# Read-back sums behind the next eviction, fetched operands behind the weights: an order for ScalarE and VectorE in a hybrid encoder layer

## The chip, the cores and the metric

The kernel runs on one core of a Trainium2 chip. The metric is the time of one execution in microseconds (us), the median of three runs. One further execution was taken by the profiler, and all rows below come from it. PE is TensorE (PEld its weight load), DVE is VectorE, ACT is ScalarE, POOL is GpSimd, SP is SyncE, which here only issues transfers.

## The reference

One layer of a streaming encoder, on 512 prompt tokens and 8 × 16 sample tokens, in float32. The lines that matter, `fox_attend` and `s5_mixer` being the attention and the state-space group:

```python
a = rms_norm(x, g_mix)
proj = a @ w_in                      # 2048 -> q, k, v, forget logits, u
...
attn = fox_attend(q, k_all, v_all, c_all[:, past:], c_all, pos_q, pos_k)
ssm, s_re_new, s_im_new = s5_mixer(u, s_re, s_im, ...)
merged = concatenate([rms_norm(attn, g_attn_out), rms_norm(ssm, g_ssm_out)], -1)
h = x + merged @ w_out               # 2048 x 2048
f = rms_norm(h, g_ffn)
h = h + (silu(f @ w_gate) * (f @ w_up)) @ w_down      # 2048 -> 5632 -> 2048
gate = sigmoid(rms_norm(h, g_ple) @ w_ple_gate)       # 2048 x 2048
h = h + gate * (p_i @ w_ple_proj)
```

Keys, values, log forget values and final states are returned too. The change touches only what comes after `merged`.

## The kernel before, in words

All 640 tokens stand on the free axis and features on the partitions. Each float32 operand is rounded to the matmul's format and its remainder is rounded as well (high and low half), and each product is three matmuls: high by high, high by low, low by high (L1243 to L1245). The part after attention and state space consists of products of the four large weight matrices with the activations: o0 to o7 (w_out), g0, u0, g1, u1, ... to u21 (w_gate, w_up), d0 to d25 (w_down, its sum over 5632 cut into pieces), p0 to p7 (w_ple_gate). Every one makes 256 output features and is computed by a seven-product scheme for 2 × 2 blocks in place of eight block products. Its sum runs over units of 512 input features; a unit is 42 matmuls of 128 × 128 weights on 320 tokens. Products o, g, u and p have four units, a d product two, three or four.

Per unit, the ring `Ring` loads 512 KB of weights on SP's queue into a staging tile `wst` (two of them), forms the four block sums `ws` on DVE (L109 to L112), rounds both to the high half `wh` on ACT (L86) and takes the low half `wl` on DVE (L87). `wh` and `wl` have two buffers, so a unit's rounding waits for the last matmul of the unit two before. `next` rounds a unit and the one after it, and `ahead`, at a product's end, the first two of the following product.

A product ends with its eviction from seven of eight PSUM banks (`strassen`): two copies on ACT (`q`, `r12`), six adds on DVE, one on POOL. In the o stage and in the last d products (`last` cells, d18 to d25) `add_h` then adds the result to the residual `o_yT` (a store that accumulates) and reads the sum back as `h`, both on POOL's queue. `done_o` or `done_h`, called one product later, scales `h` by the gain into `c` or `hc` (ACT, L1316), forms three sums of block rows in four adds (DVE, L118 to L121), stores `c` to memory (`fc_dr`, `hc_dr`, on SP's queue) and adds the squares of `h` to the norm's sums (L1291 to L1296). Later `fetch` loads such operands (`kf`, `kt`, `kh`) on POOL's queue, and `cut_next`, called after a unit, rounds one or two of them into high and low half (`cut`: ACT L1085, DVE L1086). The last o product and the last d product do their own: x7 or h5 is read on SP's queue, added on DVE, and scaled straight into the operand; `h5` and `x7` take over a buffer of the pool `R` (two buffers for the results `r`, the sums `h` and these).

On each engine the instructions run in the order that a scheduler fixes when the kernel is built. It works on a timeline that it estimates itself and takes whatever is ready by it, so code that is written later can stand earlier on an engine. `tc.issue_after(ins)`, as a context, keeps an instruction issued within it behind `ins`, on the engine of `ins`; it adds no semaphore. Before the change, none of the functions below uses it.

Of the kernel before, what the change touches and what calls it, by code (L numbers as in the profile page):

```python
# [13 lines left out]
AF = mybir.ActivationFunctionType  # L14
OP = mybir.AluOpType
# [150 lines left out]
def hybrid_step(ctx: ExitStack, tc: tile.TileContext, io):  # L166
    nc = tc.nc
# [23 lines left out]
    ring = Ring(nc, stp, units)  # L191
# [616 lines left out]
    def big(name):  # L808
        return pb_.tile([P, 2, 512], F32, tag="g", name=name, bufs=2)
# [228 lines left out]
    def hrow(j):  # L1038

        return rows(io["o_yT"], j) if j < 7 else rows(h7_dr, 0)  # L1040

    def xrow(j):
        return io["xT"][2 * j : 2 * j + 2]

    for h in range(H):
        if h:
            nc.gpsimd.dma_start(io["o_yT"][2 * (h - 1) * P : 2 * h * P, :].rearrange("(a p) n -> a p n", p=P), xrow(h - 1))
        for which in range(2):
            if h:
                ps = big(f"qk{h}{which}")  # L1050
# [63 lines left out]
    for n in range(8):  # L1114
        ps = big(f"glu{n}")
# [22 lines left out]
    for n in range(KT):  # L1138
# [4 lines left out]
        else:  # L1143
            ps = (two if n % 4 == 1 else big)(f"pj{n}")
# [33 lines left out]
    def pair(name):  # L1178
        return fo.tile([P, 2, NTOK], F32, tag="R", name=name, bufs=2)
# [29 lines left out]
        cut(k, slice(4, 7), x[:, 4:])  # L1209
        return k  # L1210

    uncut, tick = {}, [0]

    def wait_cut(k, x):

# [3 lines left out]
    def fetch(name, slot, dram, i, eng=nc.gpsimd):  # L1219
        k = kp_tile("k" + name, slot)  # L1220
        x = k[:, 1].bitcast(F32)
        eng.dma_start(x, dram[i])
        return wait_cut(k, x)

    def cut_next(n=1, age=2):

        for key in list(uncut)[:n]:
            if tick[0] - uncut[key][0] >= age:
                uncut.pop(key)[1]()

    def products(name, kps, after=None, order=None):

        ps = {i: bank(f"{name}_{i}")[:, :NH2] for i in PRODUCTS}
        n = len(kps) // 2

        def product(i, u, cut):
            a, b = PRODUCTS[i]
            wh, wl = cut
            for c in range(2):
                w = slice(c * P, (c + 1) * P)  # L1240
                k = kps[2 * u + c]
                f, l = u == 0 and c == 0, u == n - 1 and c == 1
                nc.tensor.matmul(ps[i], wh[:, a, w], k[:, 0, b], start=f, stop=False)  # L1243
                nc.tensor.matmul(ps[i], wh[:, a, w], k[:, 1, b], start=False, stop=False)  # L1244
                nc.tensor.matmul(ps[i], wl[:, a, w], k[:, 0, b], start=False, stop=l)  # L1245

        for u in range(n if order is None else n - 2):
            cut = ring.next()
            for k in kps[2 * u : 2 * u + 2]:
                if id(k) in uncut:  # L1250
                    uncut.pop(id(k))[1]()
            for i in PRODUCTS:
                product(i, u, cut)
            tick[0] += 1
            if after is not None:
                after(u)
        if order is not None:
            cuts = [ring.next() for _ in range(2)]
            for i in order:
                for u in range(2):  # L1260
                    product(i, n - 2 + u, cuts[u])
        ring.ahead()
        return ps

    def blocks(r):
        return (r[:, a, b * NH2 : (b + 1) * NH2] for a in range(2) for b in (1, 0))

    def strassen(name, kps, after=None, into=None):
        ps = products(name, kps, after)
        r = pair("r" + name) if into is None else into  # L1270
        r11, r12, r21, r22 = blocks(r)
        q = fo.tile([P, NH2], F32, tag="q", name="q" + name, bufs=1)
        tt = nc.vector.tensor_tensor
        nc.scalar.activation(q, ps[1], AF.Copy)
        tt(r11, q, ps[2], op=OP.add)
        nc.scalar.activation(r12, ps[3], AF.Copy)
        tt(q, q, ps[6], op=OP.add)
        tt(r22, q, ps[7], op=OP.add)
        tt(r12, r12, ps[5], op=OP.add)
        tt(r21, r22, ps[4], op=OP.subtract)  # L1280
        tt(r22, r22, ps[5], op=OP.add)
        nc.gpsimd.tensor_tensor(r12, r12, q, op=OP.add)
        return r

# [5 lines left out]
    def squares(s, x, first):  # L1290
        nc.scalar.activation(x, x, AF.Square)  # L1291
        if first:
            nc.vector.tensor_tensor(s, x[:, 0], x[:, 1], op=OP.add)
        else:
            nc.vector.tensor_tensor(s, s, x[:, 0], op=OP.add)
            nc.vector.tensor_tensor(s, s, x[:, 1], op=OP.add)  # L1296

    def add_h(r, j):

        nc.gpsimd.dma_start(hrow(j), r, accum_op=OP.add)  # L1300
        x = pair(f"h{j}")
        nc.gpsimd.dma_start(x, hrow(j))
        return x
# [7 lines left out]
    ssqh, ssqp = ssqa, ssqs  # L1311
# [6 lines left out]
    fk, due, f6 = [], [], []  # L1318

    def done_o(x, j):  # L1320
        c = seven(f"c{j}")
        scaled(c, x, gffn, j)
        if j < 6:
            keep(nc.vector, c, fc_dr, j)
        else:
            winograd_rows(nc.vector, c[:, :4], c[:, 4:])
            f6.append(c)
        squares(ssqh, x, j == 0)

    for j in range(8):  # L1330
        def after(u, j=j):
            if j == 7:
                if u == 2:
                    due.pop()()
                    due.append(pair("x7"))
                    nc.sync.dma_start(due[0], xrow(7).rearrange("a p n -> p a n"))
                for i in (2 * u, 2 * u + 1):
                    if i < 6:
                        fk.append(fetch(f"f{i}", i, fc_dr, i))
                cut_next(2 if u == 2 else 1, 1)  # L1340

        r = strassen(f"o{j}", mk, after)
        if j < 7 and due:
            due.pop()()
        if j < 7:
            x = add_h(r, j)
            due.append(lambda x=x, j=j: done_o(x, j))
    fk.append(whole(kp_tile("kf6", 6), f6[0]))
    x = due.pop()
# [6 lines left out]

    def after_g0(u, x=x):
        if u == 1:
            squares(ssqh, x, False)
        cut_next(1, 0)  # L1360

    tk, slots = {}, (0, 1, 2, 3, 4, 5, 6, 7)
# [1 line left out]
    def next_t():  # L1364

        u = len(tk) // 2
        if u < FT // 4:
            for i in (2 * u, 2 * u + 1):
                tk[i] = fetch(f"t{i}", slots[i % 8], tc_dr, i)
# [28 lines left out]
    due, h4 = [], []  # L1398

    def done_h(x, j):  # L1400
        c = seven(f"hc{j}")
        scaled(c, x, gple, j)
        if j in (6, 7, 4):
            winograd_rows(nc.vector, c[:, :4], c[:, 4:])
            if j == 4:
                h4.append(c)
            else:
                hk[j] = wait_cut(kp_tile(f"kh{j}", hslot[j]), c)
        else:
            keep(nc.vector, c, hc_dr, j)  # L1410
        squares(ssqp, x, j == 0)

    def next_h(j):
        hk[j] = fetch(f"h{j}", hslot[j], hc_dr, j)

    for n, (j, us, last) in enumerate(cells):
        end = n == len(cells) - 1

        def after(i, us=us, n=n, end=end):
            if end and i == 2:  # L1420
                due.pop()()
            uses[us[i]] -= 1
            if not uses[us[i]] and us[-1] < FT // 4 - 1:
                next_t()
            if n == 0 and not i:
                next_t()
            if end:
                if i == 2:
                    due.append(pair("h5"))
                    nc.sync.dma_start(due[0], hrow(5))  # L1430
                for k in ((0, 1), (2, 3), ())[i]:
                    next_h(k)
            cut_next(1, 1 if n < 2 else 2)

        r = strassen(f"d{n}", [tk[i] for u in us for i in (2 * u, 2 * u + 1)], after)
        if not last:
            nc.gpsimd.dma_start(hrow(j), r, accum_op=OP.add)
        elif not end:
            if due:
                due.pop()()  # L1440
            x = add_h(r, j)
            due.append(lambda x=x, j=j: done_h(x, j))
    hk[4] = whole(kp_tile("kh4", hslot[4]), h4[0])
    x = due.pop()
# [7 lines left out]

    def after_p0(u, x=x):
        if u == 1:
            squares(ssqp, x, False)
        cut_next(1, 0)

    for j in range(7):
# [5 lines left out]
        x = pair(f"pj{j}")  # L1464
# [5 lines left out]
    x = pair("pj7")  # L1470
# [3 lines left out]
    ps = products("p7", hk, order=(1, 2, 6, 5, 3, 7, 4))  # L1474
    z = pair("rp7")
    r11, r12, r21, r22 = blocks(z)
    q = fo.tile([P, NH2], F32, tag="q", name="qp7", bufs=1)
    tt = nc.vector.tensor_tensor
# [141 lines left out]
```

## Time and profile before

| what | value |
|---|---|
| median of 3 runs | 3013.43 us (3011.45 to 3016.4) |
| profiled execution | 3010.09 us, span 3008.0 us, mean granted clock 0.968 |
| TensorE busy | 2857.0 us, 95% of the span |
| VectorE busy | 2198.5 us, 73% |
| ScalarE busy | 1240.8 us, 41% |
| GpSimd busy | 391.3 us, 13% |
| SP's queue (q1) | 326.34 MB in 102880 packets |
| GpSimd's queue (q0) | 109.70 MB in 28240 packets |

The span is the time from the first to the last instruction. The granted clock is TensorE's, 1.00 being the upper of its two levels (2.4 GHz). In the lists of waits and in the timelines, idle time of an engine is put down to what ended it. An engine that waits costs time only where TensorE waits for it in turn.

### The profile page before, as it was taken

The page shows a single profiled execution, that of the slowest core. Times are in us where ns is not written, and L with a number is a line of the kernel's source. Part 1 is how long each engine was busy: PE and PEld are TensorE (multiplying, and loading weights), DVE is VectorE, ACT ScalarE, POOL GpSimd, SP SyncE. Part 2 cuts the span into 40 slices and gives each one's busy share as a digit, 9 for nine tenths or more (in the row PEclk, how much of TensorE's full clock was granted, in tenths as well). Part 3 has the DMA queues.
Part 4 walks back from the last instruction along what each step waited for, and adds up shares of the span by engine and source line. Part 5 has one row for each costly group of instructions (what it writes and reads, how often), then busy time and mean ns, then how long its engine had stood idle before and what let it go on. Part 6 is the DMA issues. An engine that isn't in the chain of part 4 may idle for free. (4 is left out here: it accounts for less than half of the span.)

```text
span 3008.0 us, 47275 instructions
## 1 busy us (share of the span) xinstructions
PE 2857.0 (95%) x19051; PEld 2740.2 (91%) x19051; DVE 2198.5 (73%) x3603; ACT 1240.8 (41%) x1624; POOL 391.3 (13%) x470
## 2 busy tenths in 40 slices
PE   7999999999889889999999999999999999988898
PEld 5889998887889879999999999999999999887798
DVE  7747344445777688888888888888977777767887
ACT  4333355456643453333333333333533334343433
POOL 2213300001001111110111101010111101111000
PEclk9899999999999989999999999999999999999899
DMA  6566634546545623233333233333555455546344
GB/s 226 150 182 192 217 132 163 188 156 238 199 117 165 225 94 115 100 122 100 115 100 121 94 122 103 112 114 108 206 130 169 140 146 159 157 132 194 128 137 125
DMA packets 132635, 443.26 MB, mean 147 GB/s; under 512 B 14000, under 2 KB 34576, under 8 KB 120016
## 3 DMA queue, kind: packets, MB, share of 16 engines
q1 hardware_dynamic: 102880, 326.34, 32.5%
q0 software_dynamic: 28240, 109.70, 13.1%
q10 hardware_dynamic: 1296, 4.20, 0.3%
q8 instruction: 149, 2.44, 0.3%
q14 instruction: 70, 0.57, 0.1%
HBM read 339.96 MB, written 102.16 MB: 147 GB/s over the span
## 5 line engine op out<-in xcount | busy, mean ns | idle before, releaser
L86 ACT ACTIVATE wh<-wst 128x768 fp32r<-128x768 f32 x328 | 276.5, 843 | 615.0 <-issue 284.7
L86 ACT ACTIVATE wh<-ws 128x1024 fp32r<-128x1024 f32 x328 | 345.0, 1052 | 403.6 <-DVE ws L112 403.6
L87 DVE TENSOR_TENSOR wl<-ws,wh 128x1024 fp32r<-128x1024 f32 x328 | 407.5, 1242 | 128.3 <-ACT wh L86 127.6
L87 DVE TENSOR_TENSOR wl<-wst,wh 128x768 fp32r<-128x768 f32 x328 | 329.8, 1005 | 159.7 <-ACT wh L86 159.3
L1243 PE MATMUL d<-kt,wh 128*128 128x320 f32 x1232 | 389.4, 319 | 29.7 <-ACT wh L86 20.4
L1243 PE MATMUL g<-kf,wh 128*128 128x320 f32 x1232 | 382.9, 312 | 16.1 <-ACT wh L86 7.8
L1244 PE MATMUL d<-kt,wh 128*128 128x320 f32 x1232 | 386.2, 317 | 0.0
L1244 PE MATMUL g<-kf,wh 128*128 128x320 f32 x1232 | 381.8, 311 | 0.0
L1243 PE MATMUL u<-kf,wh 128*128 128x320 f32 x1232 | 379.8, 309 | 1.0 <-ACT wh L86 1.0
L1244 PE MATMUL u<-kf,wh 128*128 128x320 f32 x1232 | 379.5, 309 | 0.0
L1245 PE MATMUL g<-kf,wl 128*128 128x320 f32 x1232 | 370.4, 311 | 2.5 <-DVE wl L87 2.5
L1245 PE MATMUL u<-kf,wl 128*128 128x320 f32 x1232 | 368.7, 309 | 0.2 <-DVE wl L87 0.2
L1245 PE MATMUL d<-kt,wl 128*128 128x320 f32 x1232 | 351.4, 317 | 10.8 <-DVE wl L87 10.6
L1243 PEld LDWEIGHTS d<-kt,wh 128*128 128x128 f32 x1232 | 239.6, 195 | 36.8 <-ACT wh L86 25.2
L1243 PEld LDWEIGHTS g<-kf,wh 128*128 128x128 f32 x1232 | 233.3, 189 | 18.5 <-ACT wh L86 9.3
L1245 PEld LDWEIGHTS d<-kt,wl 128*128 128x128 f32 x1232 | 228.0, 193 | 15.6 <-DVE wl L87 15.4
L1244 PEld LDWEIGHTS d<-kt,wh 128*128 128x128 f32 x1232 | 239.8, 195 | 0.0
L1244 PEld LDWEIGHTS g<-kf,wh 128*128 128x128 f32 x1232 | 233.4, 189 | 0.0
L1245 PEld LDWEIGHTS g<-kf,wl 128*128 128x128 f32 x1232 | 229.7, 189 | 3.7 <-DVE wl L87 3.2
L1243 PEld LDWEIGHTS u<-kf,wh 128*128 128x128 f32 x1232 | 231.2, 188 | 2.0 <-ACT wh L86 2.0
L1244 PEld LDWEIGHTS u<-kf,wh 128*128 128x128 f32 x1232 | 231.3, 188 | 0.0
L1245 PEld LDWEIGHTS u<-kf,wl 128*128 128x128 f32 x1232 | 228.1, 188 | 0.6 <-DVE wl L87 0.4
(503 smaller groups left out, 5924.4 us busy)
## 6 DMA issues: line engine op xcount, KB each, us to landing
wst<-in_w_gate SPq DMA_DIRECT2D x88, 512.0 KB
wst<-in_w_up SPq DMA_DIRECT2D x88, 512.0 KB
wst<-in_w_down SPq DMA_DIRECT2D x88, 512.0 KB
tc_dr<-t SPq DMA_DIRECT2D x22, 1120.0 KB
kt<-tc_dr POOLq DMA_DIRECT2D x22, 1120.0 KB, 8.5
wst<-in_w_qk SPq DMA_DIRECT2D x32, 512.0 KB
kc<-in_cache_k SPq DMA_DIRECT2D x16, 1024.0 KB
vc<-in_cache_v SPq DMA_DIRECT2D x16, 1024.0 KB
```

The lines of the kernel that those rows point to most:

```text
L86: a = nc.scalar.activation(wh[:, part], x, AF.Copy)
L87: b = nc.vector.tensor_tensor(wl[:, part], x, wh[:, part].bitcast(F32), op=OP.subtract)
L1243: nc.tensor.matmul(ps[i], wh[:, a, w], k[:, 0, b], start=f, stop=False)
L1244: nc.tensor.matmul(ps[i], wh[:, a, w], k[:, 1, b], start=False, stop=False)
L1245: nc.tensor.matmul(ps[i], wl[:, a, w], k[:, 0, b], start=False, stop=l)
```

## The change

`strassen` now keeps two instructions of its eviction, the second copy on ACT and the last add on DVE. A new helper `behind` runs a function with all that it issues on ACT and DVE kept behind two given instructions. It is used in four places: `done_o` and `done_h` of the previous product run behind the eviction of the product just ended; `cut_next` cuts behind the ring's latest rounding (`ring.done`: ACT's last `wh`, DVE's last `wl`); the same for the last `done_o` and `done_h` in o7 and d25; and for the last squares in g0 and p0.

```diff
@@ -1209,7 +1209,12 @@
         cut(k, slice(4, 7), x[:, 4:])
         return k
 
-    uncut, tick = {}, [0]
+    uncut, tick, evicted = {}, [0], []
+
+    def behind(ins, f):
+
+        with tc.issue_after(ins[0]), tc.issue_after(ins[1]):
+            f()
 
     def wait_cut(k, x):
 
@@ -1226,7 +1231,7 @@
 
         for key in list(uncut)[:n]:
             if tick[0] - uncut[key][0] >= age:
-                uncut.pop(key)[1]()
+                behind(ring.done, uncut.pop(key)[1])
 
     def products(name, kps, after=None, order=None):
 
@@ -1273,12 +1278,13 @@
         tt = nc.vector.tensor_tensor
         nc.scalar.activation(q, ps[1], AF.Copy)
         tt(r11, q, ps[2], op=OP.add)
-        nc.scalar.activation(r12, ps[3], AF.Copy)
+        a = nc.scalar.activation(r12, ps[3], AF.Copy)
         tt(q, q, ps[6], op=OP.add)
         tt(r22, q, ps[7], op=OP.add)
         tt(r12, r12, ps[5], op=OP.add)
         tt(r21, r22, ps[4], op=OP.subtract)
-        tt(r22, r22, ps[5], op=OP.add)
+        b = tt(r22, r22, ps[5], op=OP.add)
+        evicted[:] = a.ins, b.ins
         nc.gpsimd.tensor_tensor(r12, r12, q, op=OP.add)
         return r
 
@@ -1331,7 +1337,7 @@
         def after(u, j=j):
             if j == 7:
                 if u == 2:
-                    due.pop()()
+                    behind(ring.done, due.pop())
                     due.append(pair("x7"))
                     nc.sync.dma_start(due[0], xrow(7).rearrange("a p n -> p a n"))
                 for i in (2 * u, 2 * u + 1):
@@ -1341,7 +1347,7 @@
 
         r = strassen(f"o{j}", mk, after)
         if j < 7 and due:
-            due.pop()()
+            behind(evicted, due.pop())
         if j < 7:
             x = add_h(r, j)
             due.append(lambda x=x, j=j: done_o(x, j))
@@ -1356,7 +1362,7 @@
 
     def after_g0(u, x=x):
         if u == 1:
-            squares(ssqh, x, False)
+            behind(ring.done, lambda: squares(ssqh, x, False))
         cut_next(1, 0)
 
     tk, slots = {}, (0, 1, 2, 3, 4, 5, 6, 7)
@@ -1418,7 +1424,7 @@
 
         def after(i, us=us, n=n, end=end):
             if end and i == 2:
-                due.pop()()
+                behind(ring.done, due.pop())
             uses[us[i]] -= 1
             if not uses[us[i]] and us[-1] < FT // 4 - 1:
                 next_t()
@@ -1437,7 +1443,7 @@
             nc.gpsimd.dma_start(hrow(j), r, accum_op=OP.add)
         elif not end:
             if due:
-                due.pop()()
+                behind(evicted, due.pop())
             x = add_h(r, j)
             due.append(lambda x=x, j=j: done_h(x, j))
     hk[4] = whole(kp_tile("kh4", hslot[4]), h4[0])
@@ -1452,7 +1458,7 @@
 
     def after_p0(u, x=x):
         if u == 1:
-            squares(ssqp, x, False)
+            behind(ring.done, lambda: squares(ssqp, x, False))
         cut_next(1, 0)
 
     for j in range(7):
```

Lines after L1211 move on by five or six. Three places show what becomes of the order. In these rows the number in a name is the unit (wh, ws, wst), the product (qo3, rd7: the eviction's copies) or the operand (c2, h2, kt8).

On ACT, around the eviction of o3 (units 96 to 99; 100 and 101 are the first of o4), before:

```order
L86 ACTIVATE wh98_8568<-ws98_8570 128x1024
L1316 ACTIVATE c2_8757<-h2_8517,c_g_ffn_133 128x640 x2
L86 ACTIVATE wh99_8623<-wst99_8492 128x768
L1291 ACTIVATE h2_8517<-h2_8517 128x1280
L86 ACTIVATE wh99_8623<-ws99_8625 128x1024
L86 ACTIVATE wh100_8678<-wst100_8579 128x768
L1274 ACTIVATE qo3_8747<-o3_1_8519 128x320
L1276 ACTIVATE ro3_8746<-o3_3_8521 128x320
L86 ACTIVATE wh100_8678<-ws100_8680 128x1024
L86 ACTIVATE wh101_8733<-wst101_8634 128x768
```

and after:

```order
L86 ACTIVATE wh99_8623<-wst99_8492 128x768
L86 ACTIVATE wh99_8623<-ws99_8625 128x1024
L86 ACTIVATE wh100_8678<-wst100_8579 128x768
L86 ACTIVATE wh100_8678<-ws100_8680 128x1024
L1279 ACTIVATE qo3_8747<-o3_1_8519 128x320
L1281 ACTIVATE ro3_8746<-o3_3_8521 128x320
L1322 ACTIVATE c2_8757<-h2_8517,c_g_ffn_133 128x640 x2
L1297 ACTIVATE h2_8517<-h2_8517 128x1280
L86 ACTIVATE wh101_8733<-wst101_8634 128x768
L86 ACTIVATE wh101_8733<-ws101_8735 128x1024
```

c2 and the square of h2 stood around wh99 of o3 and now stand behind o3's two copies and in front of wh101.

On ACT, around the eviction of d7 (units 316 to 319 belong to d8, whose third and fourth unit take kt8 to kt11), before:

```order
L1085 ACTIVATE kt8_21902<-kt8_21902 128x1280
L1085 ACTIVATE kt8_21902<-kt8_21902 128x960
L86 ACTIVATE wh316_21965<-wst316_21839 128x768
L86 ACTIVATE wh316_21965<-ws316_21967 128x1024
L1085 ACTIVATE kt9_21904<-kt9_21904 128x1280
L1085 ACTIVATE kt9_21904<-kt9_21904 128x960
L86 ACTIVATE wh317_22024<-wst317_21917 128x768
L1085 ACTIVATE kt10_21961<-kt10_21961 128x1280
L1085 ACTIVATE kt10_21961<-kt10_21961 128x960
L1274 ACTIVATE qd7_22097<-d7_1_21853 128x320
L1276 ACTIVATE rd7_22096<-d7_3_21855 128x320
L1085 ACTIVATE kt11_21963<-kt11_21963 128x1280
```

and after:

```order
L86 ACTIVATE wh316_21965<-wst316_21839 128x768
L86 ACTIVATE wh316_21965<-ws316_21967 128x1024
L1085 ACTIVATE kt8_21902<-kt8_21902 128x1280
L1085 ACTIVATE kt8_21902<-kt8_21902 128x960
L86 ACTIVATE wh317_22024<-wst317_21917 128x768
L1279 ACTIVATE qd7_22097<-d7_1_21853 128x320
L86 ACTIVATE wh317_22024<-ws317_22026 128x1024
L1085 ACTIVATE kt9_21904<-kt9_21904 128x1280
L1085 ACTIVATE kt9_21904<-kt9_21904 128x960
L1281 ACTIVATE rd7_22096<-d7_3_21855 128x320
L86 ACTIVATE wh318_22083<-wst318_21976 128x768
L86 ACTIVATE wh318_22083<-ws318_22085 128x1024
```

kt8 stood in front of wh316, and kt10 and kt11 in front of wh318 and of the second half of wh317; now each pair of rows of a kt stands behind a whole unit of weights.

On SP's queue, at d25 (wst380 and later are the weights of p0), before:

```order
L60 DMA wst379_25804<-in_w_down 128x1024
L1205 DMA hc_dr_76<-hc3_25872 128x2240
L60 DMA wst380_25859<-in_w_pg 128x1024
L1430 DMA h5_26063<-o_yT 128x2x640
L60 DMA wst381_25950<-in_w_pg 128x1024
```

and after:

```order
L60 DMA wst379_25804<-in_w_down 128x1024
L1205 DMA hc_dr_76<-hc3_25872 128x2240
L1436 DMA h5_26063<-o_yT 128x2x640
L60 DMA wst380_25859<-in_w_pg 128x1024
L60 DMA wst381_25950<-in_w_pg 128x1024
```

The read of h5 has moved in front of wst380, p0's first weights.

## Rows read from the trace of the kernel before

**Rows 1.** Windows, us; PE, PEld, DVE, ACT, POOL busy; clock, DMA share, GB/s

```profile
1097.00:2161.30 1064.30, 1061.64 (x7224) 1059.12 (x7223) 881.83 (x1364) 384.67 (x461) 135.84 (x133) 1.00 0.34 114
876.50:1021.72 145.22, 131.87 (x841) 128.47 (x840) 102.92 (x186) 54.08 (x67) 14.07 (x15) 0.95 0.57 165
1021.72:1046.36 24.64, 24.64 (x170) 24.64 (x169) 19.36 (x29) 12.29 (x14) 6.01 (x9) 1.00 0.78 271
1046.36:1096.58 50.22, 33.10 (x175) 30.45 (x173) 41.72 (x61) 30.22 (x34) 6.61 (x2) 0.80 0.37 143
2161.28:2203.75 42.47, 33.09 (x170) 30.86 (x169) 37.03 (x51) 18.55 (x21) 9.89 (x9) 0.80 0.51 176
2333.11:2413.39 80.28, 77.04 (x506) 75.48 (x505) 63.83 (x106) 31.85 (x37) 9.18 (x8) 0.98 0.48 139
2536.59:2595.76 59.17, 53.68 (x338) 51.91 (x337) 46.34 (x77) 22.46 (x28) 9.23 (x8) 0.94 0.51 144
2595.76:2751.20 155.44, 137.02 (x843) 131.74 (x841) 107.57 (x187) 57.73 (x70) 18.17 (x18) 0.91 0.52 141
2726.19:2751.20 25.01, 22.08 (x129) 20.92 (x127) 17.20 (x31) 9.18 (x12) 2.97 (x3) 0.86 0.59 175
2751.20:2822.56 71.36, 51.13 (x300) 48.16 (x299) 57.42 (x89) 36.13 (x41) 7.50 (x9) 0.83 0.50 180
```

**Rows 2.** Waits: engine, line, what it waited for; total us, times, longest

```profile
ACT c L1316 <- DMA h<-o_yT: 41.2, 7, 7.7
...
ACT kt L1085 <- DMA kt<-tc_dr: 35.4, 11, 6.9
...
ACT hc L1316 <- DMA h<-o_yT: 30.7, 6, 8.7
```

**Rows 3.** Timeline, ScalarE in o2: start, duration, instruction, [idle before <-releaser]

```profile
898.60 1.55 ACT L1316 ACTIVATE c<-h,c_g_ffn 128x640 f32<-128x640 f32 x2 [7.73 <-DMA h<-o_yT]
900.06 0.83 ACT L86 ACTIVATE wh<-wst 128x768 fp32r<-128x768 f32 x1
900.79 1.25 ACT L1291 ACTIVATE h<-h 128x1280 f32<-128x1280 f32 x1
```

**Rows 4.** The same for TensorE, in o2

```profile
900.94 0.64 PE L1243 MATMUL o<-km,wh 128*128 128x320 f32 x1 [4.03 <-ACT wh L86]
```

**Rows 5.** The same for GpSimd's queue, in d24

```profile
2739.43 1.18 POOL L1300 DMA_DIRECT2D o_yT<-rd  x1 [5.11 <-DVE ws L111]
2747.61 0.75 POOL L1302 DMA_DIRECT2D h<-o_yT  x1 [7.01 <-ACT qd L1274]
```

**Rows 6.** The same for ScalarE, in d25

```profile
2752.87 1.55 ACT L1316 ACTIVATE hc<-h,c_g_ple 128x640 f32<-128x640 f32 x2 [5.52 <-DMA h<-o_yT]
```

**Rows 7.** The same for ScalarE, in d7

```profile
2322.41 2.17 ACT L1085 ACTIVATE kt<-kt 128x1280 fp32r<-128x1280 f32 x2 [5.74 <-DMA kt<-tc_dr]
```

**Rows 8.** VectorE's lines in o3: busy us, mean ns, idle before

```profile
L87 DVE TENSOR_TENSOR wl<-ws,wh 128x1024 fp32r<-128x1024 f32 x4 | 4.9, 1224 | 2.2 <-ACT wh L86 2.2
L87 DVE TENSOR_TENSOR wl<-wst,wh 128x768 fp32r<-128x768 f32 x4 | 3.8, 951 | 0.2 <-ACT wh L86 0.2
...
L1296 DVE TENSOR_TENSOR ssqa<-ssqa,h 128x640 f32<-128x640 f32 x1 | 0.8, 818 | 0.0
...
L118 DVE TENSOR_TENSOR c<-c 128x320 f32<-128x320 f32 x1 | 0.5, 492 | 5.5 <-ACT c L1316 5.5
```

**Rows 9.** Timeline of SP's queue, in d25

```profile
2764.27 0.33 SPq L60 DMA_DIRECT2D wst<-in_w_pg  x1
2771.92 0.38 SPq L1430 DMA_DIRECT2D h<-o_yT  x1
2772.42 5.33 SPq L60 DMA_DIRECT2D wst<-in_w_pg  x2
```

**Rows 10.** The same for VectorE, at p0's start

```profile
2787.46 0.42 DVE L109 TENSOR_TENSOR ws<-wst 128x256 f32<-128x256 f32 x1 [4.71 <-DMA wst<-in_w_pg]
```

**Rows 11.** The same for TensorE, at p0's start

```profile
2788.37 0.63 PE L1243 MATMUL p<-kh,wh 128*128 128x320 f32 x1 [10.58 <-ACT wh L86]
```

## The prediction

> **What bounds the kernel now.** I read the page first, then the windows by stage, then the windows product by product with the list of waits, and last the timelines of single gaps. On the page the reader is to see that TensorE is busy nearly throughout. The long gate/up stretch shows how unequal the stages are: 1061.64 of 1064.30 us are matmuls at clock 1.00 [rows 1], so nothing can be won there, and the order of its work does not change. A product of four units takes 24.64 us when nothing disturbs it (o7, [rows 1]); a three-unit product takes three quarters of that, 18.48, a two-unit product 12.32. What a stretch takes above that is lost time, and it holds the matmuls that ran at the lower clock after a gap (the clock column of rows 1 is below 1.00 in most of those stretches). The losses:
>
> - o2 to o6: 145.22 − 5 × 24.64 = 22.0 us.
> - g0, the gap ahead of it included: 50.22 − 24.64 = 25.6.
> - d0 and d1: 42.47 − 24.64 = 17.8. d8 to d10: 80.28 − 73.92 = 6.4. d16 to d18: 59.17 − 49.28 = 9.9.
> - d19 to d24 (two products of four units, four of three): 155.44 − 123.20 = 32.2.
> - d25 and p0: 71.36 − 43.12 = 28.2.
>
> Together 142 us. The list of waits names what stands ahead of the matmuls in them: ScalarE waits 41.2 us in seven places in c and 30.7 us in six places in hc for a read-back of sums (h<-o_yT), and 35.4 us in eleven places in kt for a fetched operand [rows 2]. None of these waits hurts by itself, since ScalarE is far from full. It hurts because the engines work in order and the next unit's rounding is queued behind it. The timeline of o2 shows one such chain: ScalarE waits 7.73 us for h until 898.60, does the two scalings, and only at 900.06 begins wh of the next unit [rows 3]; TensorE, idle for 4.03 us, starts again at 900.94 [rows 4].
>
> **Part 1, done_o and done_h behind the next eviction.** The order shows c2 on ScalarE moved from in front of wh99 (the last unit of o3) to behind the two copies of o3's eviction, and wh99 now stands in front. Nothing is added or removed; some 1.55 + 1.25 us on ScalarE (scalings, square) and 4 × 0.49 + 2 × 0.82 = 3.6 us on VectorE (rows of c, sums of squares; [rows 3, 8]) change place, once per product. What has to hold in the new place: the first two units of the next product are rounded in full or in part before the eviction, and its second unit is needed 6.16 us (24.64 / 4) after the product's start. Behind the eviction VectorE does in that time two adds at 0.48 and one c row (1.4 us, costed as c rows), the first wl (0.95), one sum of squares (0.82), two c rows (1.0) and the second wl (1.22): 5.4 us. The first half of the weights is there at about 2.4. So the moved work is late nowhere, if the read-back has landed. Working back from 6.16 by the scalings, the square, wh (0.83) and wl (0.95), 4.6 us in all, it must land no later than 1.6 us into the next product, that is 26.2 us after the start of the product behind which it was sent, or 20.1 for a three-unit product.
>
> In o2 it landed 898.60 − 876.50 = 22.1 us after the start [rows 1, 3], so there are 4 us in hand. In the o products I therefore expect nearly all of the 22.0 back: **20** (bounds 10, where half of each wait comes back as a gap at the next product's start, and 22).
>
> In the late three-unit products it is tight. In d24 h3, the sums of d23, was asked for at 2747.61 and was at ScalarE at 2752.87, 26.6 us after d24's start at 2726.19, since the accumulating store ahead of it was issued only at 2739.43, 13 us in [rows 1, 5, 6]. The adds of the eviction, which free that store, stood behind hc there and now stand in front of it, as in the o products; I take the store to be issued 6 us earlier, so that the sums land about at 20.6, half a microsecond over the limit. VectorE was busy for 17.20 us in d24 already [rows 1], of the 18.48 that such a product should take, so little slack is left for work that comes in another order, and I let such a product keep 2 to 4 us of loss. Of 32.2 us I take **20** (bounds 8, where only d19's and d21's losses go, and 28).
>
> **Part 2, fetched operands behind the weights.** Before, four kt cuts stand between the weights of d8, and at 2322.41 ScalarE had waited 5.74 us for one to land with wh<-wst of a nearer unit behind it [rows 7]. Now there is one cut behind each unit's weights, which are needed sooner. The wait stays, but what is queued behind it is a unit that is wanted later. In d0 and d1 this is worth less: VectorE is busy for 37.03 of 42.47 us [rows 1] with the last u eviction in it, and what goes from there (two operands, 2.2 us each on ScalarE by rows 7, and about as much on VectorE) moves to d2, whose product has room. So d0 and d1 give 6 of 17.8, d8 to d10 give 4 of 6.4 and d16 to d18 give 6 of 9.9: **16** (bounds 0, where the cuts only change places with equally urgent work, and 28).
>
> **Part 3, the two edges.** At o7 to g0 the square of h7 and the last c move behind weights; on the queues x7 is now in front of a store of c and of g0's first weights. At d25 to p0 the read of h5 goes in front of p0's first weights on SP's queue. Before, those were issued at 2764.27, well ahead of h5 at 2771.92 and of the second weights [rows 9]; VectorE waited 4.71 us for the second ones until 2787.46, TensorE's gap was 10.58 [rows 10, 11]. h5 takes over the buffer of r24, so it waits for r24's accumulating store, and the weights now wait with it; behind them on SP stand the next weights, behind their rounding on ScalarE and VectorE stand hc4 and the cuts of kh. With the store 6 us earlier, h5 is issued at about 20.7 − 6 = 14.7 us into d25; h5 and the weights one after the other at 5.3 us each (what the read-back of h3 took, [rows 5, 6]) land at 25.3, against 18.48 where TensorE wants them: a gap of about 7 where there was one of 10.6, and the second weights come right behind. I take **+2** there and **+2** at g0, where a similar wait of x7 stands against weights that landed late before too. Bounds for both: −20 (the weights arrive as late after h5 as the second ones did, 15 us after their issue, and what is queued behind goes with them, at both edges) and +15 (the wait on the first rounding goes).
>
> On this the Trainium skill, "DMA: Bandwidth & Descriptors", Queues, rings and completion order, says that each DMA engine takes turns between the queues it has work for, packet by packet, and takes a queue's own descriptors in order. The trace agrees so far: 15.0 us from the issue of the second weights at 2772.42 to their use, with kh operands on the other queue. By that rule the first weights would come 15 us after h5's issue, not 10.6, and the edge would be about 4 us worse than I have it, −2 in place of +2.
>
> **The sum.** The profiled execution took 3010.09 us, 2.1 more than its span. 20 + 20 + 16 + 4 = 60 less gives 2950. The median of the three runs, 3013.43, is 3.3 above the profiled execution, so 60 less gives **2953** on the measure of the runs.
>
> **Rivals.**
> 1. VectorE takes over as the bound. For it: 37.03 busy of 42.47 in d0 and d1, and 17.20 of the 18.48 us that d24 should take [rows 1]. Against it: the o products, where it is busy for 102.92 of 145.22 us [rows 1]. Then only the o stage gains 20 and the cuts and late products 5 each: 30, or 2983.
> 2. The edges lose, as bounded above: 20 lost at g0 and p0 against 56 won: 36, or 2977. For it: p0's first weights move behind a read that waits; against it: both edges were already waiting for weights.
> 3. Slower: the wait isn't removed but carried over the product's end. If the sums land later than 26.2 (20.1) us after the start, ScalarE stands there behind the eviction with the next unit's rounding behind it, where there is one unit of cover, 6.16 us, and not a whole product's. The 54 us of loss in o2 to o6 and d19 to d24 then stay, and each of those eleven products adds the moved 3.6 us of VectorE and 2.8 of ScalarE in front of the rounding: up to 6.4 × 11 = 70 more. With the 16 of part 2 and the 4 of part 3 won, that is 50 slower at most, 3063; half of it, where only the late products are hit and the o products gain little, gives about 3035. It decides from a landing 4 us later than o2's; the late products already stood at 26.6.
> 4. The change does nothing to the end: the waits only look like causes, and DMA or rounding behind them would have held the same matmuls. Against it is the chain at 898.60 to 900.94. Time within 6 of 3013.
>
> **How the numbers follow.** Chances: the forecast (40 to 80 less) 0.60; rival 1 0.17; rival 2 0.11; rival 3 0.07; rival 4 0.05. Range 2928 (85 less: all the upper bounds but the edges') to 2993 (20 less): the low end leaves out little, the high end rivals 3 and 4 and a part of 1. A difference under 0.2%, 6 us, cannot be told from none here. Faster by more than that: 0.60 + 0.17 + 0.11 + 0.02 of rival 4 = 0.90; within it 0.04 (rivals 3 and 4); slower 0.06.
>
> **What would show it right or wrong.** In the profile after, the waits of c and hc on h<-o_yT fall to a few microseconds, and o2 to o6 take 123 to 128 us. kt's waits on its fetch may remain, with the matmuls of d8 to d10 within 3 us of 73.92. d22 to d24 still lose 2 to 4 us each, by waits of wh on ws or wl on wh. In p0 the first gap is named wh after a wait on wst<-in_w_pg. I am wrong if new gaps of over 2 us stand 6 us after each product's start (rival 3), if VectorE has no idle time in the late products (rival 1), or if d25 and p0 take over 80 us (rival 2).

## The result, and the profile after

The changed kernel takes 2944.91 us (median of three, 2939.81 to 2945.77) against 3013.43: ratio 0.9767, 95% interval 0.9745 to 0.9789. The forecast was 2953. The profiled execution took 2944.91 us with a span of 2943.1, and TensorE is busy for 96% of it.

First the windows of the changed kernel, in the columns of [rows 1]: o2 to o6, g0, u0, d0 with d1, d2, d8 to d10, d16 to d18, d19 to d24, d24 alone, and d25 with p0.

```profile
880.48:1003.68 123.20, 123.20 (x842) 123.20 (x841) 99.08 (x181) 54.25 (x66) 14.20 (x15) 1.00 0.61 186
1028.32:1074.29 45.97, 33.66 (x178) 30.35 (x177) 43.57 (x61) 27.66 (x31) 5.07 (x2) 0.81 0.40 149
1074.29:1105.67 31.38, 27.55 (x170) 26.13 (x169) 20.89 (x37) 15.25 (x19) 0.85 (x1) 0.95 0.23 72
2142.55:2173.51 30.96, 26.76 (x171) 24.67 (x170) 29.73 (x40) 13.96 (x17) 11.12 (x9) 1.00 0.60 217
2173.51:2197.39 23.88, 21.19 (x128) 19.93 (x127) 21.38 (x33) 10.79 (x13) 2.08 (x2) 0.93 0.50 127
2308.29:2384.45 76.16, 75.20 (x507) 73.94 (x506) 62.19 (x99) 32.89 (x40) 8.06 (x8) 1.00 0.48 139
2507.64:2562.24 54.60, 52.49 (x338) 49.28 (x337) 46.49 (x73) 24.05 (x28) 8.22 (x8) 1.00 0.52 147
2562.24:2696.07 133.83, 127.02 (x843) 124.76 (x842) 108.83 (x193) 60.57 (x74) 18.38 (x18) 0.99 0.58 164
2674.70:2696.07 21.37, 19.59 (x129) 18.49 (x128) 18.75 (x36) 10.19 (x13) 3.45 (x3) 1.00 0.63 190
2696.07:2757.09 61.02, 48.73 (x301) 45.75 (x300) 54.88 (x85) 33.57 (x38) 8.52 (x9) 0.92 0.55 198
```

The reader is to see that o2 to o6 lose nothing at all: 123.20 us of TensorE in 123.20, at clock 1.00, where [rows 1] had 145.22 at 0.95. d19 to d24 went from 155.44 to 133.83, and d25 with p0 from 71.36 to 61.02. u0 now loses 6.7 us (3.2 before) and d2 5.4 (none before).

The list of waits of the changed kernel, against [rows 2]:

```profile
ACT c L1322 <- DMA h<-o_yT: 3.3, 1, 3.3
ACT hc L1322 <- DMA h<-o_yT: 3.3, 1, 3.3
```

41.2 and 30.7 us became 3.3 each. kt's wait on its fetch, 35.4 before, is no longer in the list, which goes down to totals of 2 us. The new place is seen in ScalarE's and then VectorE's timeline at the end of o3 and the start of o4 (o3's last matmul starts at 929.76, o4's first at 929.91):

```profile
926.59 0.44 ACT L1281 ACTIVATE ro<-o 128x320 f32<-128x320 f32 x1 [0.62 <-PE o L1250]
926.92 1.54 ACT L1322 ACTIVATE c<-h,c_g_ffn 128x640 f32<-128x640 f32 x2
928.49 1.28 ACT L1297 ACTIVATE h<-h 128x1280 f32<-128x1280 f32 x1
929.96 0.85 ACT L86 ACTIVATE wh<-wst 128x768 fp32r<-128x768 f32 x1 [0.19 <-PE o L1249]
```

```profile
931.44 0.95 DVE L87 TENSOR_TENSOR wl<-wst,wh 128x768 fp32r<-128x768 f32 x1
...
933.85 1.22 DVE L87 TENSOR_TENSOR wl<-ws,wh 128x1024 fp32r<-128x1024 f32 x1
```

The scalings start without a wait, in time that ScalarE had left before the buffer of wh came free. The second unit's weights are whole at 935.07, 5.2 us after o4's start. The sum before had 5.4, and TensorE wants their first half at 6.16.

### The profile page after: what moved, and what is told of

Read it like the earlier page. It is cut to its first block, busy times and chain, and to the rows that moved or that the text cites. A ratio compares the mean times of both kernels' runs of the same rounds, so it can differ in the third digit from the quotient of the medians.

```text
span 2943.1 us, 47274 instructions
## 1 busy us (share of the span) xinstructions
PE 2829.2 (96%) x19051; PEld 2717.5 (92%) x19051; DVE 2200.1 (75%) x3603; ACT 1243.8 (42%) x1624; POOL 391.9 (13%) x470
## 5 line engine op out<-in xcount | busy, mean ns | idle before, releaser
L1248 PE MATMUL d<-kt,wh 128*128 128x320 f32 x1232 | 378.2, 312 | 11.1 <-ACT wh L86 10.7
L1249 PE MATMUL d<-kt,wh 128*128 128x320 f32 x1232 | 376.7, 310 | 1.9 <-DVE kt L1086 1.9
L1250 PE MATMUL d<-kt,wl 128*128 128x320 f32 x1232 | 334.3, 312 | 4.6 <-DVE wl L87 4.0
L1248 PEld LDWEIGHTS d<-kt,wh 128*128 128x128 f32 x1232 | 232.2, 189 | 16.8 <-ACT wh L86 16.4
L1249 PEld LDWEIGHTS d<-kt,wh 128*128 128x128 f32 x1232 | 232.4, 189 | 2.5 <-DVE kt L1086 2.5
L1250 PEld LDWEIGHTS d<-kt,wl 128*128 128x128 f32 x1232 | 219.7, 188 | 8.8 <-DVE wl L87 8.2
```

## The experiments

Each ran beside the kernel before. Times of single stretches are from one profiled execution each, from the start of the last matmul ahead of a stretch to the start of its own last one, so that a gap ahead of a stretch counts in it. The starts of products given below are such edges, some 0.15 us ahead of the product's first matmul, unless the first matmul is named. In e8_whole, a second profile of the whole change, every stretch of the first table is within 0.6 us of the first profile.

**The three parts alone.** e1_sums keeps only the two `behind(evicted, ...)`, e2_cuts only the cuts behind `ring.done`, e3_edges only the last `due.pop()` and the last squares; e12_noedges has the first two. For e1:

```diff
-                behind(ring.done, uncut.pop(key)[1])
+                uncut.pop(key)[1]()
...
-                    behind(ring.done, due.pop())
+                    due.pop()()
...
-            behind(ring.done, lambda: squares(ssqh, x, False))
+            squares(ssqh, x, False)
```

> Only the first part: done_o and done_h behind the next eviction; cuts, edges and last squares as before. My theory (three parts that add up, each in its own place): o2 to o6 take 123 to 124 us (before 145.2, with the whole change 123.2), d19 to d24 130 to 138 (before 155.4, after 133.8), while d0 to d2 stay near 61, d8 to d10 near 80 and d16 to d18 near 59 as before. d25 and p0 win too, since the accumulating store is earlier: 61 to 66 (before 71.4). Sum 45 to 55 us less, ratio 0.982 to 0.985. Rival (the parts need one another: sums pushed behind an eviction only help where the cuts are out of the way): d19 to d24 stay above 145 and the ratio is above 0.988.

> Only the second part: fetched operands cut behind the latest rounding of weights. My theory: d0 to d2 take about 55 (before 61.0, after 54.8), d8 to d10 about 76 (80.3), d16 to d18 about 55 (59.2); o2 to o6 stay near 145 and d19 to d24 near 155, because the read-backs still stand in front of weights. 12 to 18 us less, ratio 0.994 to 0.996. Rival (the cuts only change places with equally urgent work, and the gain in these products came from the sums' order): ratio 0.998 to 1.0.

> Only the third part: the last done_o and done_h and the last squares behind the latest rounding. My theory: g0 to u0 and d25 to p0 gain 0 to 4 us together (ratio 0.9985 to 1.0); the 10 us that the whole change won at d25 and p0 come from the first part (the store of r24 earlier), not from these edges. Rival (the edges themselves bring the 10): 61 to 63 us for d25 and p0 in place of 71.4, ratio about 0.9965.

> The first and second part without the third. My theory: within 4 us of the whole change, ratio 0.976 to 0.979, and d25 and p0 at 60 to 65 us as with it. Rival (the edges bring the gain at p0): d25 and p0 near 71, ratio 0.980 or more.

| stretch, us | before | whole | e1 sums | e2 cuts | e3 edges | e12 sums + cuts |
|---|---|---|---|---|---|---|
| o2 to o6 | 145.4 | 123.2 | 123.2 | 147.1 | 146.1 | 123.2 |
| g0 and u0 | 78.1 | 77.4 | 71.0 | 71.8 | 76.9 | 75.4 |
| d0 to d2 | 61.0 | 54.8 | 55.9 | 54.9 | 58.1 | 54.9 |
| d8 to d10 | 80.3 | 76.2 | 82.0 | 76.2 | 80.1 | 76.2 |
| d16 to d18 | 59.2 | 54.6 | 59.2 | 55.0 | 58.6 | 54.4 |
| d19 to d24 | 155.4 | 133.8 | 126.9 | 150.0 | 154.7 | 134.8 |
| d25 and p0 | 71.4 | 61.0 | 66.6 | 72.5 | 71.8 | 65.3 |
| ratio to before | | 0.9767 | 0.9762 | 0.9901 | 0.9988 | 0.9763 |
| its 95% interval | | 0.9745 to 0.9789 | 0.9747 to 0.9777 | 0.9886 to 0.9917 | 0.9979 to 0.9997 | 0.9750 to 0.9777 |

The sums alone give the whole gain. My expectation for e1, 0.982 to 0.985, was missed on the good side, and so was that for e2 (0.994 to 0.996): the parts do not add, since 0.0238 + 0.0099 + 0.0012 is 0.035 and the whole is 0.023. By stretch one sees why. The cuts win 4 to 6 us each in d8 to d10 and d16 to d18, with or without the sums. In d19 to d24 they win 5 alone, but beside the sums they cost 8 (134.8 in e12 against 126.9 in e1), and 4.4 in g0 with u0; d25 and p0 take 1.3 less. d0 to d2 are won with either part. The waits say that each part takes away its own kind, first e1, then e2:

```profile
ACT kt L1085 <- DMA kt<-tc_dr: 35.6, 12, 6.8
ACT hc L1322 <- DMA h<-o_yT: 6.7, 1, 6.7
ACT c L1322 <- DMA h<-o_yT: 5.1, 1, 5.1
```

```profile
ACT c L1322 <- DMA h<-o_yT: 41.4, 7, 7.6
ACT hc L1322 <- DMA h<-o_yT: 30.5, 5, 8.0
```

With 35.6 us of waits of kt left, e1 is as fast as the whole change. Where e12 takes them out beside the sums, it wins 11.6 us in d0 to d2, d8 to d10 and d16 to d18, and loses 12.3 in g0 with u0 and in d19 to d24.

Not all of e1's gain is the mechanism. Of some 72 us, 22.2 come in o2 to o6, 28.5 in d19 to d24 and 4.8 in d25 and p0, where sums were moved or their stores come earlier. Another 7.1 come in g0 and u0 and 5.1 in d0 to d2, where part 1 names no instruction; the order on ScalarE and VectorE came out otherwise there all the same. Such side effects of the scheduler can stand in every column of the table, and no run here tells them from a part's own effect in these stretches.

The edges alone bring 0.1%, and e12 without them is as fast as the whole change: its d25 and p0 take 4.3 us more, but counted to the end of p1 it has 90.0 us against 89.5. Nor did they put h5 in front of p0's first weights, for in e1, e2 and e12 the order on SP's queue is the changed one, and in e3 the old one.

**Which engine's place counts.** e1 with the order kept on ScalarE alone (e4_act) and on VectorE alone (e5_dve):

```diff
-        with tc.issue_after(ins[0]), tc.issue_after(ins[1]):
+        with tc.issue_after(ins[0]):        # e4_act; ins[1] in e5_dve
```

> The first part alone, but kept behind the eviction on ScalarE only: the scalings of h stand behind the eviction's copies as before, on VectorE the rows of c stand ahead of the last adds of the eviction. My theory (what counts is where ScalarE waits for the landing): o2 to o6 take 123 to 126 us (first part whole 123.2, before 145.4); d19 to d24 127 to 134 (126.9 whole), as the store comes about 2 us later; ratio 0.976 to 0.980. Rival (what counts is that VectorE finishes the eviction first, which frees the accumulating store and the banks early): o2 to o6 stay above 134, ratio above 0.985.

> The first part alone, but kept behind the eviction on VectorE only: ScalarE's scalings stand in front of the second half of the weights of the last unit of each o product (in o4 between the two halves of wh103), though VectorE finishes the eviction first. My theory, with the landing as what decides: the sums land at about 16 us after the product's start (as in the whole change) and not at 17 to 22, the scalings are done at 17.6, and the second half of the unit's weights is needed at about 20.2, so o2 to o6 take 123 to 128. The sharper version (only ScalarE's place behind the eviction helps): 140 to 147. In d19 to d24, where hc stands between the copies, 135 to 150; ratio 0.978 to 0.985 by the first version, above 0.988 by the second.

e4: ratio 0.9812 (0.9793 to 0.9830), o2 to o6 123.2 us, d19 to d24 133.9. ScalarE's place alone brings back all of the o stage; what it misses of e1 is in the late d products and at the edge (d25 and p0 72.5, 66.6 in e1), with a ratio a little above the expected range. e5: 0.9924 (0.9903 to 0.9946), o2 to o6 132.6, d19 to d24 152.8, and c waits again:

```profile
ACT c L1322 <- DMA h<-o_yT: 35.8, 7, 8.2
```

That is between my two versions for the o stage (123 to 128, 140 to 147), on the side of the second in the ratio, and in d19 to d24 above the 135 to 150 that I gave. I had the sums land at 16 us. In o3 of e5, which begins at 906.44 and loses 4.7 us, c starts 19.9 us in, and the half of the unit's weights behind it is late:

```profile
926.36 1.55 ACT L1322 ACTIVATE c<-h,c_g_ffn 128x640 f32<-128x640 f32 x2 [5.31 <-DMA h<-o_yT]
```

**The limit on the landing.** e6_read2 reads the o stage's sums twice, one read after the other; e7_read4 four times, and holds the next product's second unit behind the scalings:

```diff
         x = pair(f"h{j}")
-        nc.gpsimd.dma_start(x, hrow(j))
+        for _ in range(reads):               # 2 in e6, 4 in e7, o stage only
+            nc.gpsimd.dma_start(x, hrow(j))
...
+            with tc.issue_after(behind(evicted, due.pop())):   # e7: the last scaling
+                ring.ahead()
```

> The whole change, with the sums of the o stage read back twice, one read after the other, so that they land 5 to 6 us later (21 to 22 us after the product's start). My theory: they may land as late as 26.2 us after the start at no cost, so o2 to o6 stay at 123 to 124 us. Rival (each microsecond of lateness costs, or the added traffic does): o2 to o6 at 135 or more.

> The whole change, with the sums of the o stage read back four times, one read after the other, and with the rounding of each next product's second unit held behind the scalings on ScalarE (the order that the whole change has by itself; the square stands behind that rounding here). The sums land 16 to 17 us later, about 32.4 after the product's start. My theory: the limit here is 24.64 + 6.16 less 3.3 for scalings, wh and wl, 27.5 us, so each of o2 to o6 loses about 5 us: 145 to 152, and the wait of c on the read-back is back in the list of waits. Rival (the change works by taking rows out of the way of rounding, whenever the sums land): 123 to 128.

e6: o2 to o6 125.1 us, 2944.86 us in one run. Only o2 and o3 lose, 0.8 and 1.1. ScalarE's timeline has c starting at

```profile
880.26 1.55 ACT L1323 ACTIVATE c<-h,c_g_ffn 128x640 f32<-128x640 f32 x2 [4.50 <-DMA h<-o_yT]
906.29 1.55 ACT L1323 ACTIVATE c<-h,c_g_ffn 128x640 f32<-128x640 f32 x2 [5.08 <-DMA h<-o_yT]
```

1.6 us after o2's first matmul (878.64) and 2.2 after o3's (904.09), against a limit of 1.6. There the sums came later than the 21 to 22 us that I expected, and the limit is off by under 1 us. From o4 on they land ahead of the eviction and nothing is lost, with twice the reads. So lateness below the limit is free here, and the added reads are too.

e7: o2 to o6 155.5, a little above what was expected, 2982.08 us in one run. Its products o2 to o6, and ScalarE's starts of c:

```profile
871.72:906.89 35.17, 27.17 (x170) 26.91 (x169) 16.55 (x31) 10.65 (x13) 5.79 (x7) 0.85 0.67 192
906.89:938.43 31.54, 27.23 (x170) 26.97 (x169) 21.10 (x37) 10.82 (x13) 5.02 (x6) 0.89 0.67 211
938.43:969.50 31.07, 26.23 (x170) 25.96 (x169) 20.73 (x38) 10.54 (x13) 5.03 (x6) 0.95 0.74 220
969.50:995.77 26.27, 24.98 (x170) 24.64 (x169) 20.66 (x37) 10.55 (x13) 5.04 (x6) 1.00 0.75 229
995.77:1027.22 31.45, 26.45 (x170) 26.18 (x169) 19.91 (x37) 10.54 (x13) 5.59 (x7) 0.95 0.76 229
```

```profile
883.85 1.55 ACT L1325 ACTIVATE c<-h,c_g_ffn 128x640 f32<-128x640 f32 x2 [14.87 <-DMA h<-o_yT]
914.46 1.55 ACT L1325 ACTIVATE c<-h,c_g_ffn 128x640 f32<-128x640 f32 x2 [8.28 <-DMA h<-o_yT]
947.41 1.55 ACT L1325 ACTIVATE c<-h,c_g_ffn 128x640 f32<-128x640 f32 x2 [9.96 <-DMA h<-o_yT]
974.93 1.55 ACT L1325 ACTIVATE c<-h,c_g_ffn 128x640 f32<-128x640 f32 x2 [6.41 <-DMA h<-o_yT]
1004.91 1.55 ACT L1325 ACTIVATE c<-h,c_g_ffn 128x640 f32<-128x640 f32 x2 [10.12 <-DMA h<-o_yT]
```

With the limit at 6.16 − 3.3 = 2.9 us after a product's start, c is late by 9.2, 4.7, 6.1, 2.5 and 6.2 us. The products lose 10.5, 6.9, 6.4, 1.6 and 6.8: the same size within 2.2 us, with the latest losing most and the least late losing least, though the three between do not keep their order. Part of the loss is matmuls at the lower clock, since the granted clock was 0.85 to 0.95 in the four products that lost most. This is the third rival of the prediction, brought about here: behind the eviction, a landing past the limit costs about a microsecond for each microsecond. In the o stage the change works because the sums land in time.

**A version that keeps both gains.** e8_whole is the whole change again. e9_early keeps the cuts behind weights only up to d18, where e2 had shown them to win; e10_early25 also in d25 and p0:

```diff
-                behind(ring.done, uncut.pop(key)[1])
+                f = uncut.pop(key)[1]
+                f() if late[0] else behind(ring.done, f)
...
+        late[0] = n >= 19                    # 19 <= n < 25 in e10_early25
```

> The whole change again, beside the two below on the same chip: ratio 0.976 to 0.978, d19 to d24 133 to 135 us, d25 and p0 60 to 66.

> The whole change, but with the cuts behind the weights only up to d18, and from d19 on placed freely as before the change. My theory (the cuts behind the weights win 14 to 15 us in d0 to d18, but from d19 on, where the sums of the eviction already stand behind, they cost 7): d0 to d2 54.9, d8 to d10 76, d16 to d18 54 to 55 as with the whole change, d19 to d24 126 to 129 as with the first part alone, d25 and p0 61 to 67: 3 to 8 us less than the whole change, ratio 0.9735 to 0.976. Rival (the parts do not add here, and the first part alone, at 0.976, is all there is): ratio 0.976 to 0.978.

> The same, with the cuts behind the weights again in d25 and p0. My theory: as e9_early up to d24, and d25 at 19 to 21 us as with the whole change (26.8 with the first part alone), d25 and p0 together 59 to 64: another 2 to 5 us, ratio 0.972 to 0.975. Rival: what d25 wins p0 loses again, so e9_early and this one are within 2 us.

| | e8 whole | e9 early | e10 early + d25 |
|---|---|---|---|
| ratio | 0.9772 | 0.9782 | 0.9785 |
| its 95% interval | 0.9755 to 0.9789 | 0.9764 to 0.9799 | 0.9768 to 0.9801 |
| d19 to d24, us | 134.3 | 130.8 | 132.0 |
| d25, us | 19.6 | 18.7 | 18.7 |
| p0, us | 40.9 | 51.1 | 49.3 |

No version is faster; the theory that the stretches' gains can be picked one by one falls. d24 gets its 2.6 us back (18.8 and 18.7 against 21.4) and d25 0.9, and p0 loses 8 to 10. In p0 of e10 ScalarE stands at

```profile
2710.84 0.84 ACT L86 ACTIVATE wh<-wst 128x768 fp32r<-128x768 f32 x1 [6.08 <-DMA wst<-in_w_pg]
2711.59 1.04 ACT L86 ACTIVATE wh<-ws 128x1024 fp32r<-128x1024 f32 x1
2712.53 0.81 ACT L1323 ACTIVATE hc<-h,c_g_ple 128x640 f32<-128x640 f32 x1
```

6.08 us for p0's second weights, with the second half of the first weights and hc4 behind them. The question is whether the transfers are late or the engines full.

**Smaller fetches at p0.** e11_smallkh is e10 with a seventh of kh0 to kh3 fetched and the rest set to zero:

```diff
+        if name[0] == "h":
+            eng.dma_start(x[:, :1], dram[i][:, :1])
+            nc.gpsimd.memset(x[:, 1:], 0.0)
```

> e10_early25 with the four fetches of kh0 to kh3 (1120 KB each on GpSimd's queue) cut to one of seven blocks, the other six set to zero on GpSimd, so p0 to p7 compute with part of their operand; the order on ScalarE, VectorE and SP's queue is nearly the same. In e10_early25 d22 to d24 were 3 to 4 us faster than with the whole change and p0 8 slower: ScalarE waited 6.08 us for p0's second weights with the second half of the first weights, hc4 and the cuts of kh behind it. My theory: these weights and the reads of sums share the transfers' bandwidth with kh0 to kh3, so with the small fetches that wait falls below 2 us, p0 takes 38 to 43 us (49.3) and d25 and p0 57 to 62 (68.0). Rival (ScalarE's and VectorE's own work between d25 and p0, about 40 us, sets the time): p0 47 to 51.

p0 took 43.9 us (49.3), d25 and p0 62.6 (68.0), 0.9 and 0.6 us more than the top of what was expected. The same instruction waits less:

```profile
2704.22 0.85 ACT L86 ACTIVATE wh<-wst 128x768 fp32r<-128x768 f32 x1 [2.58 <-DMA wst<-in_w_pg]
```

So of the 8.4 us that p0 lost against e8, 5.4 go with the size of these fetches, by one profile each: the weights beside them come sooner, and the fetches land sooner themselves. Counted from d25 to the end of p1 it is 5.5 lost (94.5 against 89.0) and 3.0 of them back (91.5). The rest, and what in the order of cuts there is best, stay open.

## Why the prediction was right, step by step

- **The o stage, 20 us predicted, 22.0 measured.** Both the mechanism and the working hold: the scalings no longer wait, the second unit's weights come 5.2 us after the start where 5.4 was worked out, and VectorE does in that time just the steps that were listed. e6 and e7 put the limit on the landing within some 2 us of where the prediction had it.
- **d19 to d24, 20 predicted, 21.6 measured.** In d24 I had the accumulating store 6 us earlier and the sums at 20.6 us after the product's start. From GpSimd's queue and ScalarE (d24 begins at 2674.70):

```profile
2680.35 1.18 POOL L1306 DMA_DIRECT2D o_yT<-rd  x1 [1.76 <-DVE hc L118]
...
2687.22 0.75 POOL L1308 DMA_DIRECT2D h<-o_yT  x1 [5.69 <-DMA o_yT<-rd]
```

```profile
2694.65 0.44 ACT L1281 ACTIVATE rd<-d 128x320 f32<-128x320 f32 x1 [1.01 <-PE d L1250]
2694.99 1.54 ACT L1322 ACTIVATE hc<-h,c_g_ple 128x640 f32<-128x640 f32 x2
```

The store is issued 5.7 us into the product (13.2 before, [rows 1, 5]), and hc starts 20.3 us in without a wait of its own, as the read landed after 6.7 us, some 19.2 us in. The 2 to 4 us that a three-unit product was to keep are 4.9, 2.9 and 2.9 in d22 to d24. What keeps them in d22 and d24 goes with the cuts of part 2: with the sums alone d22 takes 18.5 and d24 18.7 us, d23 still 21.9.

- **The fetched operands, 16 predicted, 14.8 measured in their stretches.** 11.5 in d0 and d1 (6 predicted), 4.1 in d8 to d10 (4), 4.6 in d16 to d18 (6), and 5.4 lost in d2. "The wait stays" was wrong: kt's waits are gone from the list, in e2 as well. "d2, whose product has room" was wrong too. The two products ahead of it now run 11.5 us faster, and d2's weights come late to them, as ScalarE shows. Of the 5.4 us TensorE idles 2.7, and 2.7 are matmuls at the lower clock (0.93 granted):

```profile
2176.76 0.84 ACT L86 ACTIVATE wh<-wst 128x768 fp32r<-128x768 f32 x1 [2.47 <-DMA wst<-in_w_down]
```

The whole term is not a net gain, either. e1 has none of these cuts behind weights and is as fast, since beside the sums the cuts take back in d19 to d24 and at g0 and u0 what they win elsewhere.

- **The edges, 4 predicted, 10.4 measured** (g0 4.2, u0 −3.5, d25 and p0 10.3, p1 −0.6): within its bounds, but under the wrong head. e3 shows that part 3 alone brings about nothing there. Of the 10.3 us at d25 and p0 the sums alone bring 4.8 and sums and cuts 6.0, and the rest is evened out by the end of p1. I had h5 issued at 14.7 us and the first weights at 25.3. From SP's queue, ScalarE and TensorE of the changed kernel (d25 begins at 2696.07):

```profile
2704.17 0.38 SPq L1436 DMA_DIRECT2D h<-o_yT  x1
2704.86 25.33 SPq L60 DMA_DIRECT2D wst<-in_w_pg  x4
```

```profile
2713.02 0.85 ACT L86 ACTIVATE wh<-wst 128x768 fp32r<-128x768 f32 x1 [2.21 <-DMA wst<-in_w_pg]
2715.34 1.06 ACT L86 ACTIVATE wh<-ws 128x1024 fp32r<-128x1024 f32 x1 [1.47 <-DVE ws L112]
2716.31 1.54 ACT L1322 ACTIVATE hc<-h,c_g_ple 128x640 f32<-128x640 f32 x2
2719.38 2.16 ACT L1085 ACTIVATE kh<-kh 128x1280 fp32r<-128x1280 f32 x2 [1.54 <-DMA kh<-hc_dr]
2721.45 1.25 ACT L1297 ACTIVATE h<-h 128x1280 f32<-128x1280 f32 x1
2722.61 1.25 ACT L1085 ACTIVATE kh<-hc 128x1280 fp32r<-128x1280 f32 x1
2723.77 0.83 ACT L86 ACTIVATE wh<-wst 128x768 fp32r<-128x768 f32 x1
```

```profile
2724.65 0.63 PE L1248 MATMUL p<-kh,wh 128*128 128x320 f32 x1 [6.92 <-ACT wh L86]
```

h5 went out 8.1 us into d25 and the first weights were at ScalarE at 16.9, ahead of p0's start. The 6.92 us gap looks like the 7 forecast and is another: it stands at p0's second weights, whose rounding waits behind hc4, kh0 with its landing, a square and kh4. The size was right by chance, the step wrong. On the Trainium skill's rule of turns between the queues ("DMA: Bandwidth & Descriptors", Queues, rings and completion order) I had put a price of my own, weights 15 us after h5's issue. They came 8.9 after it, so that price does not hold. e11 agrees with the rule as far as it goes: with smaller fetches on GpSimd's queue a weight load on SP's queue is waited for 2.6 us, not 6.1.

- **The rivals.** The third, the wait carried over the product's end, is real as a mechanism (e7) and did not occur, since the sums land in time. The first, VectorE as the bound, holds in d0 and d1 (busy for 29.73 of 30.96 us) and about so in d25 and p0 (54.88 of 61.02), not in the late products (18.75 of 21.37 in d24), so it took little of the gain. The second failed with its premise: p0's first weights do stand behind h5, and still came in time. The fourth falls with the waits that are gone.
- **The sum, near in part by luck.** 68.5 us came where 60 were forecast, but not from the parts as they were priced. Part 1, taken at 40, brings some 72 alone, and parts 2 and 3, taken at 20, add nothing to it that could be measured. Part 1 measured 28.5 where 20 were taken for d19 to d24, and its run is faster at g0, u0 and d0 to d2 too, where it had no term; part 2 was counted as if its gains came on top.
- **Two slips in the working.** The low end of the range, 85 less, is not the sum it is said to be: 22, 28 and 28 with the 4 of the edges make 82. And in the gate and up stretch something could be won: its 43 products need 43 × 24.64 = 1059.5 us, the stretch took 1064.3, and in e1 it took 1060.9.

## What to carry to other kernels

A wait on an in-order engine is priced by what is queued behind it, and the cure is a place where nothing urgent follows; work out from the consumer's start backwards how late the awaited data may be there, and check that it lands earlier. Such a limit can be tested by delaying the data: in the o stage lateness below it was free, and above it each microsecond cost about one. Gains of reorderings need not add: here they made 0.035 one by one and 0.023 together. And where a scheduler orders the whole kernel, an edit also changes stretches that it does not name, so run each part alone and look at the order there before crediting it with a share.

## What was not expected of the hardware

The work ahead of o0 is the same, in the same order, in all these kernels, yet o0 starts up to 10 us apart. The first matmul of o0 in the profiles of before, of the whole change, and of e1_sums:

```profile
804.68 0.31 PE L1243 MATMUL o<-km,wh 128*128 128x320 f32 x1
```

```profile
808.75 0.31 PE L1248 MATMUL o<-km,wh 128*128 128x320 f32 x1
```

```profile
798.80 0.31 PE L1248 MATMUL o<-km,wh 128*128 128x320 f32 x1
```

It is not the chip alone: e1_sums and e5_dve ran on the same one, and there o0 starts at 798.80 and 808.74. So two single spans may differ by 0.3% in a part that nobody touched; the cause stays open. Counted from o0's start to the span's end, before takes 2203.3 us, the whole change 2134.4 (2134.0 in e8) and e1 2135.9.
